# u and both gates made as Strassen column pairs behind vg, with attention outputs, normalised vg, u and gates parked in DRAM

## The chip, the cores and the metric

The kernel runs on one core of one Trainium2 chip. The metric is device time in microseconds (us) of one execution. The engines are named as in the profile: PE is the matrix engine, PEld its weight loads, DVE the vector engine, ACT the scalar engine, POOL the GpSimd engine, SP the engine that issues most DMAs; a "q" behind a name is the engine's instruction queue. POOL issues DMAs too, in its own program order.

## The reference

One transformer-like layer on x of 512 tokens by 2048 columns, in float32:

```python
h = rms_norm(x, g_mix)
q, k, v_sb, u, v_sg, gate_a, gate_b = split(h @ w_in)   # 1024,1024,1024,1024,1024,2048,2048 columns
o   = stick_breaking_attention(rms_norm(q), rms_norm(k), v_sb)     # 8 heads of 128
y_a = o @ w_oa                                                     # 1024 -> 2048
s   = gelu(u) * (W_s @ layer_norm(gelu(v_sg)) + b_s)               # mixing of 128 tokens, 8 groups
y_b = s @ w_ob                                                     # 1024 -> 2048
x   = x + (sigmoid(gate_a) * y_a + sigmoid(gate_b) * y_b) @ w_out
x   = x + square(relu(rms_norm(x) @ w_ff1)) @ w_ff2                # hidden 8192
```

## The kernel before

**Products.** Float32 operands are held as two fp32r parts, hi and lo (hi is a copy, lo the rest). A product of two such operands is three PE matmuls (`mm3`: L72 hi·hi, L73, L74), each with a moving side of up to 512 columns. Weights come by SP's queue in 512 KB pieces (`w_raw`); ACT makes `w_hi` by a copy, DVE makes `w_lo` by a subtraction (L94 and L96; L107 and L108 inside `split_to`). `w_hi` and `w_lo` share six buffers.

**Stages.** h is kept transposed (`hT`, 16 tiles of 128 rows by 512 tokens, hi and lo). In order: q, k, v for heads 0 to 3; the same for heads 4 to 7; gate a (`ga`) and y_a (`ya`) in blocks of 512 columns; `vg` (the Gelu of v_sg); u; gate b (`gb`) and y_b (`yb`); the output product `xo`; the first feed-forward product (FF1); the second. `by_token` makes a block with tokens on the partitions, `by_column` with output columns on the partitions; both take four accumulator tiles. PSUM has five such tiles for accumulators (`ps_acc`, tag "acc") and three for the rest (`ps_aux`).

**FF1** is already made in pairs of 128-column groups by a Strassen scheme over two halves of the rows, of the columns and of the tokens (`strassen_columns`). One pair of 256 columns is seven products instead of eight, on sums of weight blocks (`Sums`, made by DVE additions and by one accumulating DMA on POOL's queue, L182) and on sums of activation blocks, called factors (`y11`, `y21`, `y22`, and `m7`, `m6`, `m4`, `m5`, which `factor` makes). Six of the products use a trick of fewer matmuls: eight of 512 columns (hi and lo of the activations side by side, L214) and eight of 256 (L217). m7 has 24 of 256 columns (L72 to L74). A pair takes two accumulators (`trunk`, which carries the sum from product to product, and `side` for m7) and the three forks in `ps_aux`; ACT copies trunk into a fork (L221). The first FF1 pair is a plain one of 192 matmuls of 256 columns, since it needs no factors.

**Order.** Each engine takes its instructions in its own program order, which the tile framework's scheduler settles when the kernel is built; a waiting instruction holds everything behind it on its engine. Side work is put in a queue, `behind`: each weight piece of the main loop (`step()`) takes one entry, and `flush()` takes the rest. The attention of a half (12 entries) runs behind the next stage. `normed(tb)`, the layer norm of vg, is behind u: for each of four token blocks bn_stats (L545), r by POOL, and then for both column halves y by DVE (L554), two POOL products with the gain and bias (L556, L557), and a split into `vn`. `spatial` and `mixed` run behind gb. SBUF has 64 general slots of 128 x 512 (`slots`), 12 more until FF2 (`long`) and six weight buffers (`raws`).

## Time and profile before

| | |
|---|---|
| median of 3 runs | 2470.86 us (2469.9 to 2472.71) |
| profiled execution | 2470.69 us, its span 2469.0 us, granted clock 0.999 |
| PE busy | 2452.8 us, 99% of the span |
| DVE, ACT, POOL busy | 1625.3, 1076.4, 349.9 us |
| ga and ya | 306.8 to 588.6 us from the span's start |
| vg | 588.9 to 675.7 us |
| u | 675.9 to 762.8 us |
| gb and yb | 762.9 to 1033.0 us |
| xo | 1033.0 to 1212.8 us |
| FF1: plain pair, Strassen pairs | from 1213.0 us, from 1238.5 us to 1850.8 us |

A stage starts where the first matmul onto its tile starts. A row of a timeline gives the start in the span, the duration, the engine, the line, the operation and its tiles, and in brackets how long the engine had been idle and for whom. A matmul's row shows a longer duration than the distance to the next one, because matmuls are pipelined; the distance of starts is what one costs.

### The profile page before, as it was taken

How to read it: one execution, taken by the hardware profiler on the slowest of the kernel's cores; microseconds unless marked ns; L12 is line 12 of the kernel's file. 1: busy time of each engine (PE TensorE's matmuls, PEld its weight loads, DVE VectorE, ACT ScalarE, POOL GpSimd, SP SyncE). 2: the span in 40 equal slices, each digit the busy share in tenths (PEclk: the TensorE clock that was granted, in tenths of full speed). 3: DMA queues.
4: the chain of work that ended last, by engine and by line, in shares of the span. 5: the costliest groups of instructions: out<-in, count | busy, mean ns of one | idle time of the engine just before them, and what ended most of it. 6: DMA issues, size and time to landing. Idle time of an engine off the chain costs nothing.

```text
span 2469.0 us, 32147 instructions
## 1 busy us (share of the span) xinstructions
PE 2452.8 (99%) x12141; PEld 2078.2 (84%) x12141; DVE 1625.3 (66%) x2076; ACT 1076.4 (44%) x1521; POOL 349.9 (14%) x435
## 2 busy tenths in 40 slices
PE   9999999999999999999999999999999999999999
PEld 7888888888888888888888899888888888888887
DVE  4556463333334443334689888888888898989887
ACT  5333343122222322223377677777765443333333
POOL 0212120000030110100000000001013434312210
PEclk9999999999999999999999999999999999999999
DMA  5322322233333232434369888888895999877763
GB/s 179 94 86 70 93 77 86 94 99 97 110 101 105 93 95 94 162 128 144 97 171 235 230 232 228 225 229 229 224 290 206 309 326 295 256 227 204 248 181 95
DMA packets 349740, 416.34 MB, mean 169 GB/s; under 512 B 16992, under 2 KB 225936, under 8 KB 349584
## 3 DMA queue, kind: packets, MB, share of 16 engines
q1 hardware_dynamic: 290256, 320.41, 40.4%
q0 software_dynamic: 59040, 93.34, 16.5%
q8 instruction: 95, 1.56, 0.3%
q10 hardware_dynamic: 288, 0.52, 0.1%
q14 instruction: 61, 0.50, 0.1%
HBM read 347.10 MB, written 67.11 MB: 168 GB/s over the span
## 4 chain that ended last, share of the span: by engine, by line
PE 95%; DVE 2%; DMA 1%; issue 1%; ACT 0%; POOL 0%; DVEq 0%; SPq 0%; POOLq 0%; ACTq 0%
PE q L72 10%; PE q L73 10%; PE q L74 10%; PE q L214 7%; PE fork L214 7%; PE fork L217 4%; PE q L217 4%; PE xo L74 2%; PE xo L72 2%; PE xo L73 2%; PE gb L72 2%; PE gb L73 2%; PE gb L74 2%; PE ga L72 2%; PE ga L74 2%; PE ga L73 2%
## 5 line engine op out<-in xcount | busy, mean ns | idle before, releaser
L107 ACT CAST w_hi<-w_raw 128x1024 fp32r<-128x1024 f32 (+1 forms) x443 | 465.3, 1051 | 506.7 <-PE q L73 310.3
L108 DVE TENSOR_TENSOR w_lo<-w_raw,w_hi 128x1024 fp32r<-128x1024 f32 (+1 forms) x443 | 537.5, 1217 | 113.0 <-ACT w_hi L107 107.1
L96 DVE TENSOR_TENSOR w_lo<-w_raw,w_hi 128x1024 fp32r<-128x1024 f32 x211 | 261.7, 1240 | 523.7 <-ACT w_hi L94 519.7
L94 ACT CAST w_hi<-w_raw 128x1024 fp32r<-128x1024 f32 x211 | 221.9, 1052 | 656.7 <-PE ga L73 99.6
L73 PE MATMUL q<-w_lo,ys 128*128 128x512 f32 x896 | 349.1, 390 | 1.1 <-DVE w_lo L108 1.1
L74 PE MATMUL q<-w_hi,ys 128*128 128x512 f32 x896 | 348.6, 389 | 0.0
L72 PE MATMUL q<-w_hi,ys 128*128 128x512 f32 x896 | 312.1, 389 | 0.9 <-ACT w_hi L107 0.9
L182 POOL DMA_DIRECT2D w_raw<-in_w_ff_dram x58 | 80.9, 1396 | 905.7 <-DVE m L749 341.6
L73 PEld LDWEIGHTS q<-w_lo,ys 128*128 128x128 f32 x896 | 168.2, 188 | 37.5 <-DVE w_lo L108 2.8
L72 PEld LDWEIGHTS q<-w_hi,ys 128*128 128x128 f32 x896 | 168.1, 188 | 36.3 <-ACT w_hi L107 1.3
L74 PEld LDWEIGHTS q<-w_hi,ys 128*128 128x128 f32 x896 | 168.2, 188 | 34.8
L214 PE MATMUL q<-ys,w_hi 128*128 128x512 f32 x744 | 193.1, 395 | 2.5 <-ACT fork L221 2.5
L214 PE MATMUL fork<-ys,w_hi 128*128 128x512 f32 x744 | 186.0, 392 | 0.0
L214 PEld LDWEIGHTS fork<-ys,w_hi 128*128 128x128 f32 x744 | 136.4, 189 | 26.1
L846 POOL DMA_DIRECT2D ys<-store x224 | 127.8, 602 | 179.6 <-PE q L74 117.6
L214 PEld LDWEIGHTS q<-ys,w_hi 128*128 128x128 f32 x744 | 132.6, 190 | 24.5 <-ACT fork L221 2.7
L892 DVE SCALAR_TENSOR_TENSOR total<-q,plus,total 128x512 f32<-128x512 f32 x180 | 130.8, 743 | 0.4 <-PE q L74 0.4
L217 PEld LDWEIGHTS fork<-ys,w_lo 128*128 128x128 f32 x744 | 101.6, 190 | 7.2
L217 PEld LDWEIGHTS q<-ys,w_lo 128*128 128x128 f32 x744 | 101.1, 190 | 7.5
L217 PE MATMUL fork<-ys,w_lo 128*128 128x256 f32 x744 | 104.1, 282 | 0.0
L217 PE MATMUL q<-ys,w_lo 128*128 128x256 f32 x744 | 103.3, 281 | 0.0
L72 PE MATMUL xo<-w_hi,mT_hi 128*128 128x512 f32 x256 | 100.1, 393 | 0.0
(283 smaller groups left out, 4827.9 us busy)
## 6 DMA issues: line engine op xcount, KB each, us to landing
w_raw<-in_w_ff_dram SPq DMA_DIRECT2D x256, 512.0 KB, 5.5
w_raw<-in_w_in_dram SPq DMA_DIRECT2D x143, 512.0 KB, 3.5
ys<-store POOLq DMA_DIRECT2D x224, 256.0 KB, 6.9
w_raw<-in_w_ff_dram POOLq DMA_DIRECT2D x58, 512.0 KB, 6.9
store<-ys_hi SPq DMA_DIRECT2D x90, 256.0 KB, 4.4
store<-ys_lo SPq DMA_DIRECT2D x90, 256.0 KB, 5.4
w_raw<-in_w_out_dram SPq DMA_DIRECT2D x32, 512.0 KB, 3.7
store<-ys SPq DMA_DIRECT2D x44, 256.0 KB, 6.2
```

The costliest lines, as they stand in the source:

```text
L72: nc.tensor.matmul(o, lhsT=lh[0], rhs=rh[0], start=start, stop=False, **kw)
L73: nc.tensor.matmul(o, lhsT=lh[0], rhs=rh[1], start=False, stop=False, **kw)
L74: nc.tensor.matmul(o, lhsT=lh[1], rhs=rh[0], start=False, stop=stop, **kw)
L94: nc.scalar.copy(out=hi, in_=raw)
L96: nc.vector.tensor_tensor(out=lo, in0=raw, in1=f32(hi), op=ALU.subtract)
L107: nc.scalar.copy(out=hi, in_=src)
L108: state["lo"] = nc.vector.tensor_tensor(out=lo, in0=src, in1=f32(hi), op=ALU.subtract)
L182: nc.gpsimd.dma_start(out=self.w21, in_=self.blocks[1, 1], accum_op=ALU.add)
L214: nc.tensor.matmul(o, lhsT=hi[:, k, :], rhs=rhs[name][k], start=name == "y11" and k == 0, stop=False, skip_group_check=True)
L217: nc.tensor.matmul(o[:, :HS], lhsT=lo[:, k, :], rhs=rhs[name][k][:, :HS], start=False, stop=k == KH - 1, skip_group_check=True)
L846: nc.gpsimd.dma_start(out=f32(t), in_=store[f][HELD.index(name), p])
L892: nc.vector.scalar_tensor_tensor(out=a, in0=o, scalar=part, in1=a, op0=ALU.mult, op1=ALU.add)
```

## The change

u, gate a and gate b (5120 columns) are made in one run of 20 pairs of 256 columns that follows vg: a plain pair first, then 19 Strassen pairs, by the functions that FF1 uses (`plain_pair`, `strassen_pair`, now shared). For that `hT` is split so that the hi and lo of 256 tokens lie side by side in one tile, which makes them the factors y11 to y22 as they are. The other four factors of each of eight k come from `gate_factors`, which reads the whole h back from DRAM (`held_h`, written by `save` behind k). Their four entries follow the 12 of the second half's attention, all behind vg. The attention's outputs (`held_o`), the normalised vg (`held_v`), u and the gates (`held_g`) are written to DRAM and fetched by POOL's queue (`fetched`) when ya and yb need them. `normed` is now queued ahead of the run of pairs, `spatial` and `mixed` run behind ya.

**ACT at the end of vg.** `vg` L527 (L608 after) is the Gelu that empties a vg accumulator. Before:

```order
L94 CAST w_hi_5041<-w_raw_5039 128x1024 [waits DMAHW6_49,DVE_49,PE_49]
L527 ACTIVATE vg_4964<-vg_4720,rstd_109 128x512 [waits PE_49]
L527 ACTIVATE vg_4966<-vg_4721,rstd_109 128x512 [waits PE_49]
L527 ACTIVATE vg_4968<-vg_4722,rstd_109 128x512 [waits PE_49]
L94 CAST w_hi_5096<-w_raw_5094 128x1024 [waits DMAHW7_49,DVE_49,PE_49]
L527 ACTIVATE vg_4970<-vg_4723,rstd_109 128x512 [waits PE_49]
L94 CAST w_hi_5151<-w_raw_5149 128x1024 [waits DMAHW0_49,DVE_49,PE_49]
```

After (`ys` from `whole` are the hi parts of the factors):

```order
L94 CAST w_hi_3882<-w_raw_3880 128x1024 [waits DMAHW7_49,PE_49,Activation_49]
L110 ACTIVATE ys_3519<-whole_3516 128x256 [waits DMASW5_49,DVE_49]
L107 CAST ys_3523<-whole_3516 128x256 [waits DVE_49]
...
L107 CAST ys_3693<-whole_3676 128x256 [waits DMASW6_49,Activation_49]
L608 ACTIVATE vg_3696<-vg_3218,rstd_109 128x512 [waits Activation_49]
L608 ACTIVATE vg_3698<-vg_3219,rstd_109 128x512 [waits Activation_49]
L608 ACTIVATE vg_3700<-vg_3220,rstd_109 128x512 [waits Activation_49]
L608 ACTIVATE vg_3702<-vg_3221,rstd_109 128x512 [waits PE_49,Activation_49,Pool_49]
L94 CAST w_hi_3965<-w_raw_3963 128x1024 [waits DMAHW0_49,PE_49]
```

The Gelus of the second half stood between two weight copies; now 24 copies for the factors of six k stand between the weight copy and them.

**PE from the end of vg.** u_3712 and u_3713 are the two accumulators of the plain pair, q_4072 is the trunk of the first Strassen pair, q_4257 and q_4258 are trunk and side of the second:

```order
L74 MATMUL vg_3221<-w_hi_3628,hT_582 128x512
L72 MATMUL u_3712<-hT_149,w_hi_3716 128x256 [waits Activation_49]
...
L74 MATMUL u_3712<-hT_462,w_lo_3884 128x256
L72 MATMUL u_3713<-hT_149,w_hi_3716 128x256 [waits Activation_49]
...
L74 MATMUL u_3713<-hT_582,w_lo_3967 128x256
L214 MATMUL q_4072<-hT_149,w_hi_4074 128x512 [waits Activation_49]
...
L217 MATMUL q_4257<-hT_567,w_lo_4260 128x256
L72 MATMUL q_4258<-ys_3443,w_hi_4282 128x256 [waits DVE_49,Activation_49]
```

The second block of the plain pair waits for ACT at its first matmul, and the side tile of the second pair waits for DVE and ACT. The four vg accumulators and u_3712 are five tiles, as are u_3712, u_3713, q_4072, its side tile and q_4257.

**DVE at the emptying of u.** Before, at the end of `normed` (y is L554, u L566):

```order
L96 TENSOR_TENSOR w_lo_5374<-w_raw_5370,w_hi_5372 128x1024 [waits DMAHW2_49,PE_49,Activation_49]
L108 TENSOR_TENSOR vn_lo_5193<-y_5188,vn_hi_5192 128x512 [waits Activation_49]
L554 TENSOR_SCALAR y_5196<-vg_4970,mv_5182,r_5186 128x512
L96 TENSOR_TENSOR w_lo_5404<-w_raw_5400,w_hi_5402 128x1024 [waits DMAHW3_49,PE_49,Activation_49]
L108 TENSOR_TENSOR vn_lo_5201<-y_5196,vn_hi_5200 128x512 [waits Activation_49]
L566 TENSOR_TENSOR u_5324<-u_4980,rstd_b_110 128x512
L566 TENSOR_TENSOR u_5327<-u_4981,rstd_b_110 128x512
```

After (y is L635; L647 empties the plain pair, L275 the first Strassen pair):

```order
L108 TENSOR_TENSOR vn_lo_3875<-y_3870,vn_hi_3874 128x512 [waits Activation_49]
L635 TENSOR_SCALAR y_3943<-vg_3214,mv_3937,r_3941 128x512 [waits DMASW6_49]
...
L108 TENSOR_TENSOR vn_lo_4031<-y_4026,vn_hi_4030 128x512 [waits DMASW3_49,Activation_49]
L635 TENSOR_SCALAR y_4036<-vg_3702,mv_4020,r_4024 128x512 [waits DMASW4_49]
L108 TENSOR_TENSOR vn_lo_4041<-y_4036,vn_hi_4040 128x512 [waits Activation_49]
L647 TENSOR_TENSOR act_4046<-u_3712,rstd_b_110 128x512 [waits DMASW7_49,DMASW5_49]
L647 TENSOR_TENSOR act_4050<-u_3713,rstd_b_110 128x512 [waits DMASW6_49]
L275 TENSOR_TENSOR act_4060<-act_4060,fork_4054 128x256 [waits Activation_49]
```

The emptying of u_3712 stands behind the last `vn_lo` of `normed`, as that of u_4980 did; what is new is that PE's side tile of the second Strassen pair hangs on it, and that the weight pieces of a Strassen pair lie between the halves.

**POOL at the start of ya.** From the last accumulating weight load on; oT are the attention outputs, vn and u the inputs of `mixed`:

```order
L182 DMA w_raw_7394<-in_w_in_dram 128x8x128 [waits DMAHW0_49,DMASW0_49,DMAHW7_49,DVE_49,Activation_49]
L477 DMA oT_7581<-held_o_137 128x512 [waits PE_49]
...
L477 DMA oT_7593<-held_o_137 128x512 [waits DMASW0_49,PE_49]
L477 DMA oT_7595<-held_o_137 128x512 [waits DMASW1_49,PE_49]
L477 DMA oT_7597<-held_o_137 128x512 [waits DMASW2_49,PE_49]
L477 DMA vn_7680<-held_v_138 128x512 [waits DMASW3_49]
...
L477 DMA vn_7694<-held_v_138 128x512 [waits DMASW2_49]
L477 DMA u_7696<-held_g_139 128x512 [waits DMASW3_49]
...
L477 DMA u_7702<-held_g_139 128x512 [waits DMASW6_49]
```

Nothing of this stood on POOL's queue before; the waits on PE are for slots that the last pairs still read.

```diff
+    def plain_pair(wap, c0, ys, name):
+        o = [acc(name) for _ in range(2)]
+        for kt in range(0, KT, 4):
+            hi, lo = weight(wap, kt, c0, 2 * P)
+            for c in range(2):
+                for k in range(4):
+                    a = [part[:, k, c * P:(c + 1) * P] for part in (hi, lo)]
+                    for half in range(2):
+                        y = ys["y" + "12"[k % 2] + "12"[half], (kt + k) // 2]
+                        mm3(o[c][:, half * HS:(half + 1) * HS], a, sides(y),
+                            kt + k + half == 0, kt + k == KT - 1, skip_group_check=True)
+            step()
+        return o
...
+    def strassen_pair(wap, c0, ys, forks, loaded=True):
+        act = [slot("act"), slot("act")]
+        a11, a12, a21, a22 = (act[c][:, half * HS:(half + 1) * HS] for c in range(2) for half in range(2))
...
+    def new_forks(y):
+        forks = {}
+        for name in ("y21", "m4", "y22"):
+            forks[name] = aux("fork")
+            nc.tensor.matmul(forks[name], lhsT=y[:, :P], rhs=y, start=True, stop=True)
+        return forks
+    SIGNS = (1.0, -1.0)
...
+                parts = [both[:, 0, :], both[:, 1, :]]
             else:
-                parts = split(t, "hT", gT[:, k:k + 1], long if k < LONG // 2 else slots)
+                parts = [slot("hT", F32R, long if k < LONG // 2 else slots) for _ in range(2)]
+            for half, part in enumerate(parts):
+                split_to(part[:, :HS], part[:, HS:], t[:, half * HS:(half + 1) * HS], gT[:, k:k + 1])
             hT.append(parts)
...
+    held_h = dram.tile([KT, P, W], F32, name="held_h")
+    held_o = dram.tile([HEADS, 2, P, W], F32, name="held_o")
+    held_v = dram.tile([2, NTB, 2, P, W], F32, name="held_v")
+    held_g = dram.tile([(SGW + 2 * D) // P, P, W], F32, name="held_g")
     scale = float(P) ** -0.5
+    def fetched(src, name, dt=F32, pool=slots):
+        t = slot(name, dt, pool)
+        nc.gpsimd.dma_start(out=f32(t) if dt is F32R else t, in_=src)
+        return t
+    def save(k):
+        t = slot("whole")
+        for half, part in enumerate(hT[k]):
+            hi, lo = (f32(x) for x in sides(part))
+            nc.vector.tensor_tensor(out=t[:, half * HS:(half + 1) * HS], in0=hi, in1=lo, op=ALU.add)
+        nc.gpsimd.dma_start(out=held_h[k], in_=t)
...
-            oT[half * 4 + h] = split(o, "oT")
+            for i, part in enumerate(split(o, "oT")):
+                nc.gpsimd.dma_start(out=held_o[half * 4 + h, i], in_=f32(part))
...
+        if half == 0:
+            behind.extend([lambda k=k: [save(k + i) for i in range(4)] for k in range(0, KT, 4)])
...
-    GA = 3 * SBW + 2 * SGW
-    merged_a = []
-    ga = [gate(GA, "ga"), gate(GA + W, "ga")]
-    flush()
...
-        by_column(w_oa[0], j * W, lambda k: oT[k], SBW // P, evac_a, "ya")
...
+    hy = {}
+    def moved(k):
+        for half, part in enumerate(hT[k]):
+            name = "y" + "12"[k % 2] + "12"[half]
+            if LONG // 2 <= k < LONG // 2 + RAWH and name != "y12":
+                t = slot("hT", F32R)
+                nc.sync.dma_start(out=f32(t), in_=f32(part))
+                part = t
+            hy[name, k // 2] = part
+    def gate_factors(k):
+        whole = [fetched(held_h[2 * k + i], "whole") for i in range(2)]
+        for name in ("m7", "m6", "m4", "m5"):
+            factor(hy, whole, k, name, -1.0 if name in ("m7", "m4") else None)
+    behind.extend([lambda k=k: (moved(2 * k), moved(2 * k + 1), moved(2 * k + 2), moved(2 * k + 3),
+                                gate_factors(k), gate_factors(k + 1)) for k in range(0, KT // 2, 2)])
...
-            vn[tb, half] = split(y, "vn")
+            for i, part in enumerate(split(y, "vn")):
+                nc.gpsimd.dma_start(out=held_v[half, tb, i], in_=f32(part))
...
-    u = []
-    for half in range(2):
-        def evac_u(c, o):
-            t = slot("u")
...
-        by_column(win, 3 * SBW + half * W, hT_of, KT, evac_u, "u")
...
+    def gated(n, act, func, signs, inside):
+        for c, (t, sign) in enumerate(zip(act, signs)):
+            a = t if inside else slot("act")
+            nc.vector.tensor_tensor(out=a, in0=t, in1=rstd_b, op=ALU.mult)
+            nc.scalar.activation(out=a, in_=a, func=func, scale=sign)
+            nc.sync.dma_start(out=held_g[n + c], in_=a)
+    US, GA = 3 * SBW, 3 * SBW + 2 * SGW
+    order = [(US + n * P, n, AF.Gelu) for n in range(0, SGW // P, 2)]
+    order += [(GA + n * P, SGW // P + n, AF.Sigmoid) for n in range(0, 2 * D // P, 2)]
+    forks = None
+    for c0, n, func in order:
+        if forks is None:
+            gated(n, plain_pair(win, c0, hy, "u"), func, (1.0, 1.0), False)
+            flush()
+            forks = new_forks(hy["y11", 0])
+        else:
+            gated(n, strassen_pair(win, c0, hy, forks), func, SIGNS, True)
+    oT = [[fetched(held_o[h, i], "oT", F32R, long if h < LONG // 2 else slots) for i in range(2)]
+          for h in range(HEADS)]
...
+    def gates(which, j):
+        n = SGW // P + which * (D // P) + j * 4
+        return [fetched(held_g[n + c], "gate") for c in range(4)]
...
+    def fetch_mix(half):
+        for tb in range(NTB):
+            vn[tb, half] = [fetched(held_v[half, tb, i], "vn", F32R) for i in range(2)]
+        u.extend(fetched(held_g[half * 4 + g], "u") for g in range(4))
...
+    behind.extend([lambda: (spatial(0), fetch_mix(0)), lambda: spatial(1)])
+    behind.extend([lambda g=g: (mixed(g), fetch_mix(1) if g == 1 else None) for g in range(GROUPS)])
+    merged_a = []
+    ahead = gates(0, 0)
+    for j in range(D // W):
+        g, ahead = ahead, gates(0, j + 1) if j + 1 < D // W else gates(1, 0)
...
+        by_column(w_oa[0], j * W, lambda k: oT[k], SBW // P, evac_a, "ya")
     flush()
-    behind.extend([lambda: spatial(0), lambda: spatial(1)])
-    behind.extend([lambda g=g: mixed(g) for g in range(GROUPS)])
...
-    gb = [gate(GA + D, "gb"), gate(GA + D + W, "gb")]
...
-        g = gb.pop(0) if gb else gate(GA + D + j * W, "gb")
-        flush()
+        g, ahead = ahead, gates(1, j + 1) if j + 1 < D // W else None
```

More of the change, by code (lines that the diff above doesn't have):

```diff
@@ new lines, in tile_hybrid_layer, with __init__, __getitem__, evac @@
+    class Late:
+        def __init__(self, ys, name):
+            self.ys, self.name = ys, name
+        def __getitem__(self, k):
+            return self.ys[self.name, k]
+    def strassen_pair(wap, c0, ys, forks, loaded=True):
+        act = [slot("act"), slot("act")]
+        a11, a12, a21, a22 = (act[c][:, half * HS:(half + 1) * HS] for c in range(2) for half in range(2))
+        def evac(name, o, side):
+            a = {"y21": a11, "m4": a21, "m5": a22, "y22": a12}[name]
+            nc.scalar.copy(out=a, in_=o[:, :HS])
+            state["evac"] = nc.vector.tensor_tensor(out=a, in0=a, in1=o[:, HS:], op=ALU.add)
+            if name in ("m4", "m5"):
+                state["evac"] = nc.vector.tensor_tensor(out=a, in0=a, in1=side, op=ALU.add)
+        strassen_columns(wap, c0, {name: Late(ys, name) for name in NAMES}, forks, evac, loaded=loaded)
+        return act
@@ L419, in evac @@
             n.append(raw)
[L421 removed]
+        by_token(win, c0 + half * W, hT_at, KT, evac, name)
         def head(h):
@@ L803, in last_factors, with hidden @@
             factor(hs, x2T[2 * k:2 * k + 2], k, name, -1.0 if name == "m4" else None)
-    class Late:
-        def __init__(self, name):
-            self.name = name
-        def __getitem__(self, k):
-            return hs[self.name, k]
-    rhs = {name: Late(name) for name in NAMES}
+    def hidden(p):
+        act = strassen_pair(w_ff1[0], p * 2 * P, hs, forks, p < pairs - 1)
+        for a, sign in zip(act, SIGNS):
+            nc.scalar.activation(out=a, in_=a, func=AF.Relu, scale=sign)
+        return act
     last_factors(0)
@@ L822, in tile_hybrid_layer @@
     behind.extend([lambda k=k: two(k) for k in range(1, KT // 2, 2)])
-    def hidden(p):
-        act = [slot("relu"), slot("relu")]
-        a11, a12, a21, a22 = (act[c][:, half * HS:(half + 1) * HS] for c in range(2) for half in range(2))
-        def evac(name, o, side):
-            a = {"y21": a11, "m4": a21, "m5": a22, "y22": a12}[name]
-            nc.scalar.copy(out=a, in_=o[:, :HS])
-            state["evac"] = nc.vector.tensor_tensor(out=a, in0=a, in1=o[:, HS:], op=ALU.add)
-            if name in ("m4", "m5"):
-                state["evac"] = nc.vector.tensor_tensor(out=a, in0=a, in1=side, op=ALU.add)
-        strassen_columns(w_ff1[0], p * 2 * P, rhs, forks, evac, loaded=p < pairs - 1)
-        for a, sign in zip(act, (1.0, -1.0)):
-            nc.scalar.activation(out=a, in_=a, func=AF.Relu, scale=sign)
-        return act
     def fetch(f, name):
@@ L848, in fetch @@
         return ts
-    forks = {}
-    for name in ("y21", "m4", "y22"):
-        forks[name] = aux("fork")
-        nc.tensor.matmul(forks[name], lhsT=hs["y11", 0][:, :P], rhs=hs["y11", 0], start=True, stop=True)
+    forks = new_forks(hs["y11", 0])
     pairs = DFF // (2 * P)
```

75 lines of the change are left out of this document (26 added, 49 removed).

## The prediction

> **What bounds the kernel now.** I read the page's busy table and slices first, then the waits of PE, then the tiles of the stages that go, then single matmuls.
>
> ```profile
> PE 2452.8 (99%) x12141; PEld 2078.2 (84%) x12141; DVE 1625.3 (66%) x2076; ACT 1076.4 (44%) x1521; POOL 349.9 (14%) x435
> PE   9999999999999999999999999999999999999999
> DVE  4556463333334443334689888888888898989887
> PE 95%; DVE 2%; DMA 1%; issue 1%; ACT 0%; POOL 0%; DVEq 0%; SPq 0%; POOLq 0%; ACTq 0%
> ```
>
> PE is busy in every slice and is 95% of the chain of waits. In FF1 (slices 20 to 29) DVE is 80 to 90% busy and PE still never waits.
>
> ```profile
> PE gp L300 <- DMA gm<-in_g_mix_dram: 5.9, 1, 5.9
> PE q L214 <- ACT fork L221: 2.5, 1, 2.5
> PE q L73 <- DVE w_lo L108: 1.1, 4, 0.3
> PE q L72 <- ACT w_hi L107: 0.9, 1, 0.9
> ```
>
> These are all of PE's waits but three of 0.2 us: 5.9 us at the start, some 5 us after. So the time is PE's matmuls, and a change is worth the matmul time that it removes less every wait that it gives PE. The pitch of a matmul, from u and from an FF1 pair:
>
> ```profile
> L72 PE MATMUL u<-hT_hi,w_hi x104: 389/389/389, 675.9 to 762.3; 128*128 128x512 f32 x104
> L74 PE MATMUL u<-hT_hi,w_lo x104: 389/389/389, 676.3 to 762.7; 128*128 128x512 f32 x104
> 700.15 0.39 PE L74 MATMUL u<-hT_hi,w_lo 128*128 128x512 f32 x1
> 700.38 0.39 PE L72 MATMUL u<-hT_both,w_hi 128*128 128x512 f32 x1
> ...
> 1500.57 0.28 PE L72 MATMUL q<-ys,w_hi 128*128 128x256 f32 x1
> 1500.69 0.28 PE L73 MATMUL q<-ys,w_hi 128*128 128x256 f32 x1
> 1520.19 0.28 PE L72 MATMUL q<-ys,w_hi 128*128 128x256 f32 x1
> ```
>
> A matmul of 512 columns costs 0.226 us (u: 384 of them in 86.9 us), one of 256 costs 0.12. From m7 of one pair to m7 of the next are 19.62 us.
>
> **Matmuls removed.** u and the gates are ten blocks of 512 columns at 43.45 us, 434.5 us. In their place come a plain pair, 192 x 0.12 = 23.0, three forks, 3 x 0.226 = 0.7, and 19 pairs at 19.62 = 372.8: 396.5 us. Removed: 38.0 us. I take the FF1 pair as it is, with its waits for loads, sums and forks, because DVE has less to do here: an FF1 pair also makes and stores the factors for FF2, and a gate pair has two products with `rstd_b` of some 0.7 us instead. Attention, `mixed` and the output products keep their matmuls.
>
> **First new wait: the plain pair.** Time t runs from its first matmul. By the order, 75 matmuls of u_3712 come before u_3713, so PE is there at t = 9.0. The fifth accumulator comes free by the Gelu of vg_3218, on ACT behind 24 copies for the factors of six k; ahead of these stands `w_hi_3882`, which waits for the last vg products, so that the six k start at about t = 2 (copy 1.05, `w_lo` 1.2 after it). How DVE and ACT hand factors over is seen at FF1's start (under it the Gelu, the weight copy and rest, and a product with `rstd_b`):
>
> ```profile
> 1244.52 0.75 DVE L655 TENSOR_TENSOR x2T<-x2T 128x256 f32<-128x256 f32 x2
> 1245.30 0.41 ACT L107 CAST ys<-x2T 128x256 fp32r<-128x256 f32 x1 [2.66 <-DVE x2T L655]
> 1245.74 0.42 DVE L108 TENSOR_TENSOR ys<-x2T,ys 128x256 fp32r<-128x256 f32 x1 [0.47 <-ACT ys L107]
> 1246.08 0.42 DVE L111 SCALAR_TENSOR_TENSOR ys<-x2T,ys 128x256 fp32r<-128x256 f32 x1
> 676.82 0.68 ACT L527 ACTIVATE vg<-vg,rstd 128x512 f32<-128x512 f32 x1
> ...
> L107 ACT CAST w_hi<-w_raw 128x1024 fp32r<-128x1024 f32 (+1 forms) x443 | 465.3, 1051 | 506.7 <-PE q L73 310.3
> L108 DVE TENSOR_TENSOR w_lo<-w_raw,w_hi 128x1024 fp32r<-128x1024 f32 (+1 forms) x443 | 537.5, 1217 | 113.0 <-ACT w_hi L107 107.1
> L566 DVE TENSOR_TENSOR u<-u,rstd_b x8: 677/682/692, 722.2 to 763.1; 128x512 f32<-128x512 f32 x8
> ```
>
> Difference, copy, rest, each waiting for the one before: 0.42 + 0.41 + 0.42 and 0.03 at each hand-over, 1.3 us. m7, m6 and m4 of a k follow each other like this, since each difference overwrites the half-tile that the last one's parts are read from; m5 is independent and costs its last step: about 4.1 us a k, 24.5 for six. The Gelu ends at 2 + 24.5 + 0.68 = 27.1, and PE waits 18.1 us. From below: where nothing waits DVE starts one such instruction per 0.34 us (1245.74 to 1246.08), eight a k, 2.7 x 6 = 16.1, and the wait is 9.7. I take the long one, since the overwriting is in the code.
>
> **Second new wait: m7 of the second Strassen pair.** Its side tile needs u_3712 emptied, on DVE behind the last half of `normed`. Before, one half went like this:
>
> ```profile
> 683.54 0.68 DVE L108 TENSOR_TENSOR vn_lo<-y,vn_hi 128x512 fp32r<-128x512 f32 x1
> 684.14 0.54 DVE L554 TENSOR_SCALAR y<-vg,mv,r 128x512 f32<-128x512 f32 x1
> 684.81 1.29 POOL L556 TENSOR_TENSOR y<-y,lng 128x512 f32<-128x512 f32 x1 [2.89 <-issue]
> 686.18 1.30 POOL L557 TENSOR_TENSOR y<-y,lnb 128x512 f32<-128x512 f32 x1
> 687.70 0.62 ACT L107 CAST vn_hi<-y 128x512 fp32r<-128x512 f32 x1
> 690.26 1.29 POOL L556 TENSOR_TENSOR y<-y,lng 128x512 f32<-128x512 f32 x1 [2.79 <-DVE y L554]
> L545 DVE BATCH_NORM_STATS2 st<-vg x8: 677/694/695, 630.0 to 678.6; 128x6 f32<-128x512 f32 x8
> L182 POOL DMA_DIRECT2D w_raw<-in_w_ff_dram x58 | 80.9, 1396 | 905.7 <-DVE m L749 341.6
> L846 POOL DMA_DIRECT2D ys<-store x224 | 127.8, 602 | 179.6 <-PE q L74 117.6
> ```
>
> POOL's two L556 rows are 5.45 us apart, but that is the pace of u's weight pieces (24 x 0.226 = 5.43), whose copies stand between the halves on ACT; a half's own chain is 0.54 + 0.13 + 1.37 + 1.30 + 0.62 + 0.68 and small gaps, 4.7 us. Now POOL also issues two stores for each half, 0.6 us each; the one behind `vn_lo` comes before the next half's product: 5.3 us. Eight are 42.4; two accumulating loads of 1.4 and two fetches of oT of 0.6 stand among them: 46.4 us. It starts with the Gelus at 27.1; four bn_stats of 0.69 with their small followers, r and y take about 5: 32.4. So u_3712 is empty at about t = 78.8.
>
> Without any wait PE would be at this m7 at t = 23.0 + 0.7 + 19.6 + 2.8 (the pair's first product, eight of each kind) = 46.1. The two waits together cost 78.8 - 46.1 = 32.7 us: 18.1 in the plain pair and the rest, 14.6, here. From below, with both chains at their fast bound: 2 + 16.1 + 0.7 + 5.3 + 8 x 4.7 + 0.7 = 62.4, a cost of 16.3. From above: if each half also waits for a weight copy and its rest, 1.05 + 1.22, it takes 7.6, u_3712 is empty at t = 97.2, and the cost is 51.1. I take 32.7, since PE's long wait lets the weight pieces run ahead, and keep POOL's issues, which stand in the order.
>
> **A cold clock after the wait.** PE's first matmuls of the run, after 5.94 us without work:
>
> ```profile
> 5.94 0.25 PE L300 MATMUL gp<-ident,gm 16*128 16x16 f32 x1 [5.94 <-DMA gm<-in_g_mix_dram]
> 9.04 0.63 PE L72 MATMUL q<-w_hi,hT_hi 128*128 128x512 f32 x1
> 9.47 0.63 PE L73 MATMUL q<-w_lo,hT_hi 128*128 128x512 f32 x1
> 10.62 0.40 PE L72 MATMUL q<-w_hi,hT_hi 128*128 128x512 f32 x1
> ```
>
> They stand 0.43 us apart until 10.4 and 0.23 after: from 6.1 on some 4.3 us at about half speed, 2.1 us lost. If PE falls back so after 14 and 18 us of waiting, each wait costs 0 to 2.1 more. After the first one it hides in the second, whose end DVE and POOL set. I add 2.1 once. [...]
>
> **The start of ya.** ya used oT from SBUF; now three halves of oT, eight of vn and four of u are fetched only when the last pair lets go of the slots, and `merged_a`, which empties ya's accumulators, stands on DVE behind `sT` of `mixed`.
>
> ```profile
> ys<-store POOLq DMA_DIRECT2D x224, 256.0 KB, 6.9
> GB/s 179 94 86 70 93 77 86 94 99 97 110 101 105 93 95 94 162 128 144 97 171 235 230 232 228 225 229 229 224 290 206 309 326 295 256 227 204 248 181 95
> L621 POOL TENSOR_TENSOR smix<-smix,u x8: 1287/1293/2135, 783.7 to 830.1; 128x512 f32<-128x512 f32 x8
> ```
>
> The fetch of u is the twelfth: 12 x 0.6 + 6.9 = 14.1 us after the last pair; then POOL's product 1.29, a copy 0.62 and a rest 0.68. Two groups of `merged_a` stand behind such a step of 2.6 us: 5.2 us, my value. Below: 0, if PE has four free accumulators' work by then. Above: 3.9 MB of fetches and 4.2 MB of w_oa at the 230 GB/s of FF1 take 35 us, the last needed about 24 us after the pair: 11 us.
>
> **The rest** is hidden. `save` adds 32 DVE instructions of 0.42 us behind k and v, where DVE is 40 to 60% busy; `hT` in twice as many instructions adds 0 to 0.5 us at the very start; the stores of u and gates are two issues a pair on SP. Were SP's stores late, weight loads behind them would be late: see the rivals.
>
> **Sum**, on the profiled execution's 2470.7 (span 2469.0 and 1.7 around it; the median is 0.2 above): - 38.0 + 32.7 + 2.1 + 5.2 = + 2.0, so 2472.7; I say 2472 us.
>
> **Rivals.**
>
> *Shorter waits, faster.* Both chains run near their fast bound: 16.3 instead of 32.7, 2456 us. For it: DVE and ACT at FF1's start did run 0.34 us apart for a while, since there independent factors alternated. Against it: the overwriting, and POOL's stores.
>
> *No waits at all*, since the order is not what decides or the tile comes free otherwise: 2472.7 - 32.7 - 2.1 = 2438 us. Against it: the order names ACT and DVE at exactly these two matmuls, and there are five tiles.
>
> *DRAM decides at ya, slower.* The fetches share the DMA engines with w_oa, and the upper bound of 11 us holds: 2472.7 + 5.8 = 2478.5. It decides once the last oT or vn lands more than 24 us after the last pair. For it: 6.9 us of landing was measured at 230 GB/s. Against it: the slices of FF2 reach 326 GB/s.
>
> **Numbers.** A measurement of this kernel tells 0.2%, 4.9 us, from no change: 2465.9 to 2475.8. The forecast, no change, 0.38; shorter waits 0.28; no waits 0.04; DRAM at ya 0.22; 0.08 for a wait I have not seen (a late store on SP's queue among them), slower. Faster 0.32, same 0.38, slower 0.30. Likeliest alone: 2464 to 2478. The range, which reaches into both neighbours: 2454 to 2486.
>
> **What would show it.** In the changed profile: PE's waits with one of about 18 us at the first u_3713 matmul behind ACT's Gelu, and one of about 15 at an m7, behind DVE's L647; matmuls 0.24 us apart instead of 0.12 for some 4 us after them; 19.6 us from m7 to m7 from the third pair on; POOL's products of `normed` 5 to 7 us apart; a few us of waiting for `merged_a` at ya. I am wrong if the first wait is under 12 us (then the factors don't chain), if pairs are longer than 20 us, or if ya loses more than 11.

## The result, and the profile after

The changed kernel takes 2494.17 us (median of 5 runs, 2492.42 to 2495.54) against 2469.9 us of the kernel before (5 runs, 2467.83 to 2472.71): a ratio of 1.0097, 95% interval 1.0082 to 1.0112. It is slower by 24 us; the forecast was 2472 us and its range ended at 2486. The profiled execution has a span of 2492.4 us and a granted clock of 0.987 (before: 2469.0 and 0.999).

The busy table of the changed kernel, and its slices of PE and of the granted clock:

```profile
PE 2428.3 (97%) x12696; PEld 2087.2 (84%) x12696; DVE 1848.0 (74%) x2416; ACT 1196.2 (48%) x1759; POOL 467.9 (19%) x590
PE   9999998699999989999999999999999999999999
PEclk9999999899999989999999999999999999999999
```

PE now has three slices that are not full: 7 and 8 (374 to 498 us), where the run of pairs starts, and 15 (872 to 935 us), where ya does. The clock dips in two of the three. The largest waits of PE (who waited for whom; us in total, times, the longest):

```profile
PE q L72 <- DVE act L647: 18.6, 1, 18.6
PE u L72 <- ACT vg L608: 15.6, 1, 15.6
PE gp L366 <- DMA gm<-in_g_mix_dram: 5.9, 1, 5.9
PE ya L72 <- DVE merged_a L737: 5.0, 2, 2.5
PE mix L717 <- DVE smix L723: 3.9, 2, 2.2
PE wsT L685 <- DMA ws<-in_w_spatial_dram: 2.6, 1, 2.6
PE q L214 <- ACT fork L221: 2.5, 1, 2.5
PE u L72 <- DMA hT<-hT_both: 2.1, 1, 2.1
PE ya L74 <- DVE w_lo L96: 1.1, 1, 1.1
```

All waits together are 58.9 us, before 11.0: 47.9 more. PE's busy time fell by 24.5 us and not by the 38.0 of the removed matmuls, which leaves 13.5 us. -38.0 + 47.9 + 13.5 = +23.4, as the span grew; this is only busy and idle time added up again, so it has to close. That the 13.5 us are matmuls at a lower clock is seen in their starts: the slow stretches named below make up some 12 of it. So two things have to be explained, the waits and the slow matmuls.

Where they lie follows from a few starts on PE. The first matmul of the plain pair is at 415.07 us. The two large waits, in PE's timeline (start, duration; in brackets the idle time before and for whom):

```profile
423.77 0.35 PE L72 MATMUL u<-hT,w_hi 128*128 128x256 f32 x1 [2.10 <-DMA hT<-hT_both]
...
443.73 0.58 PE L72 MATMUL u<-hT,w_hi 128*128 128x256 f32 x1 [15.60 <-ACT vg L608]
444.11 0.42 PE L73 MATMUL u<-hT,w_hi 128*128 128x256 f32 x1
...
449.27 0.28 PE L74 MATMUL u<-hT,w_lo 128*128 128x256 f32 x1
449.39 0.28 PE L72 MATMUL u<-hT,w_hi 128*128 128x256 f32 x1
...
501.76 0.55 PE L72 MATMUL q<-ys,w_hi 128*128 128x256 f32 x1 [18.64 <-DVE act L647]
```

The plain pair ends its first wait at t = 28.7 and m7 of the second Strassen pair starts at t = 86.7, where 46.1 was the figure without any wait: 40.6 us lost up to there. From then on the pairs run as in FF1: m7 starts again at 523.8 us and its 24 L72 matmuls of three pairs reach to 565.5, two pitches of 19.6 us. ya starts at 851.7 and xo at 1057.7 us, a stretch of 206.0 us; less its waits and slow matmuls it is 187 (below). xo came at 1033.0 us before, so all of the difference lies ahead of it.

### The profile page after: what moved, and what is told of

Same layout as the page of the kernel before. It is cut to its first block, busy times and chain, and to the rows that moved or that the text cites. A ratio compares the mean times of both kernels' runs of the same rounds, so it can differ in the third digit from the quotient of the medians.

```text
span 2492.4 us, 34437 instructions
## 1 busy us (share of the span) xinstructions
PE 2428.3 (97%) x12696; PEld 2087.2 (84%) x12696; DVE 1848.0 (74%) x2416; ACT 1196.2 (48%) x1759; POOL 467.9 (19%) x590
## 4 chain that ended last, share of the span: by engine, by line
PE 61%; DVE 1%; DMA 0%; issue 0%; ACT 0%; POOL 0%; DVEq 0%
PE q L72 9%; PE q L73 9%; PE q L74 9%; PE q L214 7%; PE fork L214 7%; PE fork L217 4%; PE q L217 4%; PE xo L72 2%; PE xo L74 2%; PE xo L73 2%; PE yb L74 1%; PE yb L73 1%; PE yb L72 1%; PE ya L72 1%; PE ya L73 1%; PE ya L74 1%
## 5 line engine op out<-in xcount | busy, mean ns | idle before, releaser
L107 ACT CAST w_hi<-w_raw 128x1024 fp32r<-128x1024 f32 (+1 forms) x576 | 604.8, 1050 | 661.1 <-PE q L73 339.7
L108 DVE TENSOR_TENSOR w_lo<-w_raw,w_hi 128x1024 fp32r<-128x1024 f32 (+1 forms) x576 | 704.9, 1227 | 169.9 <-ACT w_hi L107 160.2
L96 DVE TENSOR_TENSOR w_lo<-w_raw,w_hi 128x1024 fp32r<-128x1024 f32 x135 | 168.9, 1251 | 243.1 <-ACT w_hi L94 239.1
L94 ACT CAST w_hi<-w_raw 128x1024 fp32r<-128x1024 f32 x135 | 141.8, 1050 | 373.0 <-issue 78.3
L72 PE MATMUL q<-w_hi,ys 128*128 128x512 f32 x896 | 312.0, 389 | 0.9 <-ACT w_hi L107 0.9
L214 PE MATMUL q<-ys,w_hi 128*128 128x512 f32 x1048 | 268.4, 393 | 2.5 <-ACT fork L221 2.5
L214 PE MATMUL fork<-ys,w_hi 128*128 128x512 f32 x896 | 224.9, 393 | 0.0
L214 PEld LDWEIGHTS q<-ys,w_hi 128*128 128x128 f32 x1048 | 186.9, 189 | 34.1 <-ACT fork L221 2.7
L72 PEld LDWEIGHTS q<-w_hi,ys 128*128 128x128 f32 x896 | 168.1, 188 | 36.2 <-ACT w_hi L107 1.3
L217 PEld LDWEIGHTS q<-ys,w_lo 128*128 128x128 f32 x1048 | 142.5, 190 | 10.4
L217 PE MATMUL q<-ys,w_lo 128*128 128x256 f32 x1048 | 145.7, 282 | 0.0
L72 PE MATMUL q<-ys,w_hi 128*128 128x256 f32 x400 | 114.4, 286 | 18.6 <-DVE act L647 18.6
```

Of the source, the lines that this page charges most:

```text
L72: nc.tensor.matmul(o, lhsT=lh[0], rhs=rh[0], start=start, stop=False, **kw)
L94: nc.scalar.copy(out=hi, in_=raw)
L96: nc.vector.tensor_tensor(out=lo, in0=raw, in1=f32(hi), op=ALU.subtract)
L107: nc.scalar.copy(out=hi, in_=src)
L108: state["lo"] = nc.vector.tensor_tensor(out=lo, in0=src, in1=f32(hi), op=ALU.subtract)
L214: nc.tensor.matmul(o, lhsT=hi[:, k, :], rhs=rhs[name][k], start=name == "y11" and k == 0, stop=False, skip_group_check=True)
```

## The experiments

The reasons to test were these. The order theory (A): the two large waits are only a matter of where the factors and `normed` are queued, and go when these are queued later. Its rival (B): DVE, ACT and POOL have to get through this work before the pairs can run on, so the wait moves to the next one in need of it. After the first four runs a third was formed (C): the 64 general slots are full, and what empties an accumulator waits for slots that `normed` holds until its halves are stored. Beside them: what the DVE and POOL do to each other, what the clock costs, and what holds ya. Runs without an interval are single executions; the kernel before measured 2468.55 to 2469.48 on the same chips, and the changed kernel scatters by up to 1.8 us around its median.

**Late factors (1).** Only the factors of k = 0 and 1 stay behind vg, the other six are queued behind the plain pair, ahead of `normed`:

```diff
-                                gate_factors(k), gate_factors(k + 1)) for k in ...
+                                gate_factors(k) if k == 0 else None, ...
+    behind.extend([lambda k=k: (gate_factors(k), gate_factors(k + 1)) for k in range(2, KT // 2, 2)])
     behind.extend([lambda tb=tb: normed(tb) for tb in range(NTB)])
```

> Edit: only the factors of the first two k are made behind vg; those of the other six are queued behind the plain pair, so that the Gelus which empty vg come ahead of them. Theory A (each wait is a matter of what stands ahead of an emptied tile, and each costs its own length and some 2.5 us of half clock after it): the 15.6 us wait in the plain pair and its slow matmuls go; the emptying of u now stands behind two halves of the layer norm and not eight, so that the 18.6 us wait goes too; the first m7 waits about 5 us for its last factor: 2452 to 2462 us. Theory B (the 24 us of factors and 50 us of layer norm have to pass DVE, ACT and POOL ahead of the pairs in any case, the waits only move): 2480 to 2494 us, with a long wait at the first or second m7.

2501.44 us, above both forecasts. The plain pair has no wait left, and PE waits later and longer. The largest of these waits:

```profile
PE q L214 <- ACT fork L221: 35.8, 4, 29.2
PE q L72 <- ACT ys L110: 5.4, 3, 2.0
```

and ACT's timeline there, the last copy of `normed` and then the emptying of the first Strassen pair (L274), behind which PE's next fork (L221) stands:

```profile
514.36 0.62 ACT L107 CAST vn_hi<-y 128x512 fp32r<-128x512 f32 x1 [4.23 <-POOL y L639]
514.88 0.36 ACT L274 COPY act<-fork 128x256 f32<-128x256 f32 x1
515.14 0.38 ACT L274 COPY act<-q 128x256 f32<-128x256 f32 x1
515.41 0.66 ACT L274 COPY act<-fork 128x256 f32<-128x256 f32 x2
516.06 0.57 ACT L221 COPY fork<-q 128x512 f32<-128x512 f32 x1
```

The emptying stands behind all eight halves; that its tiles (`act`) come from slots which are free only when halves of vn are in DRAM is argued here, and tried in the run with the norm in place. Theory A falls: moved work takes its wait along.

**Late norm (2), and both late (3).** `normed` behind the emptying of the plain pair; then also the late factors:

```diff
-    behind.extend([lambda tb=tb: normed(tb) for tb in range(NTB)])
...
             forks = new_forks(hy["y11", 0])
+            behind.extend([lambda tb=tb: normed(tb) for tb in range(NTB)])
```

> Edit: the layer norm of vg is queued behind the emptying of the plain pair, not ahead of it. Theory A: the wait of 18.6 us at the second m7 goes with its 2.5 us of half clock, the wait in the plain pair stays: 2470 to 2476 us. Theory B: the layer norm's instructions stand in the second and third pair's way and PE waits for weight rests instead, in sum as long: 2485 to 2494 us.

> Edit: both of the above. Theory A: both waits gone but for about 5 us at the first m7: 2450 to 2460 us, no more than 5 us below the first edit alone. Theory B: 2475 to 2494 us.

2494.2 and 2496.86 us, both just above what B allowed. In the first of them u is emptied at once and the wait for L647 is gone, but PE waits 22.3 us for forks (longest 14.9) where it had waited 2.5; in the other 31.7 us. No place in the order removes the wait.

**Norm in place.** The y of `normed` overwrites vg, which nothing else reads: eight slots fewer.

```diff
-            y = slot("y")
+            y = t
```

> Edit: on the changed kernel, the layer norm writes y over its vg tile and takes no slot of its own; all instructions stay. The first four runs let the wait of PE move and not vanish, so two theories stand. Theory B (throughput: DVE, ACT and POOL must pass factors and layer norm first): no gain, 2491 to 2496 us. Theory C (the 64 slots of SBUF are full of hT, 32 factors and vg, so that the tiles into which u and the first pair are emptied come free only when halves of the layer norm have been stored): with one slot less per half the emptying stands behind six halves, not eight, and the second wait of 18.6 us loses some 8 to 10: 2482 to 2488 us.

2480.29 us, 14 less, of which 7.6 lie in the run of pairs (from the first matmul of u to that of ya 429.0 us instead of 436.6) and 3.7 at ya. No PE wait for L647 is left; two of PE's waits, and DVE's row of the eight y:

```profile
PE u L72 <- ACT vg L608: 16.4, 1, 16.4
PE u L74 <- DVE w_lo L96: 7.7, 1, 7.7
```

```profile
445.48 13.12 DVE L635 TENSOR_SCALAR vg<-vg,mv,r 128x512 f32<-128x512 f32 x8
```

This is what theory C says of the second wait. The change takes no operation away; with slots at hand DVE makes all eight y in a row, where in the changed kernel each y stands behind the `vn_lo` of the half ahead of it (the orders shown under "The change" have it: y and the emptying of u wait for DMAs of POOL's queue there, DMASW, and for none in the kernel before). 7.7 us come back as a new wait: `w_lo` of the plain pair now stands on DVE behind those y, which take 13.1 us beside POOL's products where eight at their usual 0.54 would take 4.3.

**Norm on DVE.** The two products with gain and bias go from POOL to DVE:

```diff
-            nc.gpsimd.tensor_tensor(out=y, in0=y, in1=lng[half], op=ALU.mult)
-            nc.gpsimd.tensor_tensor(out=y, in0=y, in1=lnb[half], op=ALU.add)
+            nc.vector.tensor_tensor(out=y, in0=y, in1=lng[half], op=ALU.mult)
+            nc.vector.tensor_tensor(out=y, in0=y, in1=lnb[half], op=ALU.add)
```

> Edit: on the changed kernel, the layer norm's two products (gain, bias) are made by DVE instead of POOL. In the changed kernel's trace DVE's 128x1024 subtractions take 2.2 to 2.3 us where they lie beside a POOL product, 1.2 elsewhere, and POOL's products 1.9 to 2.15 beside them, 1.29 alone. If the two engines slow each other there, the 2.2 us rows vanish and the second wait shrinks by 6 to 10 us, also since a half needs no hand-over to POOL: 2482 to 2488 us. If the stores' slots alone decide, 2490 to 2495 us.

2484.68 us, 9.5 less; the second wait is 10.0 us instead of 18.6. DVE makes such a product in 0.69 us, so the run alone does not tell a faster engine from an undisturbed one; but its subtractions of 128x1024 are back at 1.22 us. Why POOL's products are slow is seen in the changed kernel, DVE's timeline and then POOL's over the same 6 us:

```profile
464.17 1.21 DVE L108 TENSOR_TENSOR w_lo<-w_raw,w_hi 128x1024 fp32r<-128x1024 f32 x1
465.41 2.20 DVE L186 TENSOR_TENSOR w_raw<-w_raw 128x1024 f32<-128x1024 f32 x1
467.53 2.31 DVE L108 TENSOR_TENSOR w_lo<-w_raw,w_hi 128x1024 fp32r<-128x1024 f32 x1
```

```profile
464.65 1.88 POOL L637 TENSOR_TENSOR y<-y,lng 128x512 f32<-128x512 f32 x1
466.61 2.15 POOL L638 TENSOR_TENSOR y<-y,lnb 128x512 f32<-128x512 f32 x1
```

By these rows they take turns here. POOL's first product begins at 464.65 and ends at 466.53, 1.15 us after DVE's subtraction (465.38); DVE's next one, from 465.41, ends 1.08 us after that product (467.61 after 466.53); POOL's second ends 1.15 us after it (468.76), and DVE's last 1.08 us after that. In the kernel before such a subtraction takes 1.22 (DVE) and such a product 1.29 us (POOL), 0.14 us more than these distances. In the best version below there are no such turns.

**Warm clock.** 70 matmuls whose result nothing reads stand behind the first matmuls of the plain pair, so that PE is idle for less of its first wait:

> Edit: on the changed kernel, 70 matmuls of 512 columns without a use (15.8 us) stand in PE's order behind the first 24 of the plain pair, so that PE works through most of what was its first wait. Nothing else is changed; the tile that they write is read by nobody. If the half clock comes from PE's idling, the granted clock stays at 1.00 through the plain pair, its matmuls behind the wait stand 0.12 us apart and not 0.21, and only the second wait is followed by slow ones; the time stays within 2 us of the changed kernel (2492 to 2496), since the end of the second wait is set by the layer norm and its stores, not by PE. If the slow clock has another cause, the matmuls stay 0.21 apart.

2491.64 us, 2.5 less. The first wait is 3.3 us. Up to it and for 1 us behind it the clock stays up (matmuls 0.12 us apart), then it falls all the same (0.21 us apart), from 444.1 to 447.5 us:

```profile
443.09 0.39 PE L72 MATMUL u<-hT,w_hi 128*128 128x256 f32 x1 [3.32 <-ACT vg L612]
443.31 0.28 PE L73 MATMUL u<-hT,w_hi 128*128 128x256 f32 x1
...
444.51 0.41 PE L73 MATMUL u<-hT,w_hi 128*128 128x256 f32 x1
444.73 0.41 PE L74 MATMUL u<-hT,w_lo 128*128 128x256 f32 x1
```

So the expectation that no slow matmul follows the first wait was missed: after 3.3 us of waiting they stand 0.21 us apart here too. The second wait is 18.8 us and ends at t = 86.6 (86.7 in the changed kernel), when DVE has emptied the tile; slow matmuls ahead of it cost nothing, as the prediction had it. The 2.5 us lie elsewhere, 2.2 of them between ya and xo.

**The start of ya: mixing later, weights earlier.** In one run `spatial` and `mixed` stand three steps further behind ya's fetches; in the other the spatial weights `ws` and `bs` are asked for at the ninth of the 20 pairs, not behind the last one (n counts groups of 128 columns, two a pair, so n = 16 is not the seventeenth pair, as the expectation has it; `ws` is issued at 607.9 us instead of 848.2):

```diff
-    behind.extend([lambda: (spatial(0), fetch_mix(0)), lambda: spatial(1)])
+    behind.extend([lambda: fetch_mix(0), lambda: None, lambda: None, lambda: spatial(0), lambda: spatial(1)])
```

```diff
+        if n == 16:
+            load_ws()
```

> Edit: on the changed kernel as it is, the fetches for the spatial mixing are queued as before, but the spatial weights and the mixing follow three steps of ya later. If ya loses its 20 us by the order in which the mixing's short chain (PE, DVE, POOL, ACT, DVE) stands ahead of the emptying of ya, and by the late spatial weights, half of it goes: 2480 to 2486 us. If the DMA engines set the pace there (they move 370 to 400 GB/s for 35 us), nothing changes: 2491 to 2496 us.

> The changed kernel with one edit: the spatial weights and biases (ws, bs) are asked for at the seventeenth Strassen pair and no longer behind the last one's ref. The wait wsT <- DMA ws of 2.6 us must go. If the late weights are what costs the start of ya its 20 us (everything of the mixing stands behind them in TensorE's order), the time is 2483 to 2489. If it is the order of the mixing's own steps (sT, mix, merged_a, each released by VectorE a step late), only the wait itself goes, and the time is 2490 to 2494.

Later mixing: 2484.79 us, 9.4 less; ya to xo 196.0 instead of 206.0 us; the wait for `smix` is gone, that for `merged_a` is 3.7, that for `ws` 3.4. Early weights, in 4 runs: 2489.05 us (2487.73 to 2490.42; to before 1.0081, 1.0065 to 1.0096), 5.1 less; ya to xo 202.0; the wait for `ws` is gone, those for `merged_a` (5.0) and `smix` (4.3) are as they were. Half of the 5.1 is the wait itself, and the time falls between the two forecasts. So the larger part is the order of the mixing's own steps, each of which PE asks for before DVE has it, and late weights the smaller.

The clock has its part in it. The windows of PE in the changed kernel (stretch, its length, busy us and matmuls, granted clock, DMA share, GB/s):

```profile
850.00:860.00 10.00, 10.00 (x52) 1.00 1.03 378
860.00:870.00 10.00, 7.40 (x29) 0.83 1.04 376
870.00:880.00 10.00, 8.92 (x42) 1.00 1.04 396
...
890.00:900.00 10.00, 6.46 (x21) 0.66 0.61 203
...
920.00:930.00 10.00, 5.25 (x26) 0.85 0.37 115
930.00:940.00 10.00, 10.00 (x38) 0.81 0.06 24
```

Busy time by the missing clock, 7.40 x 0.17 + 6.46 x 0.34 + 5.25 x 0.15 + 10.00 x 0.19, is 6.1 us; with 12.6 of waits 18.7 are lost, and 187.3 remain. In the last version below the same sum gives 196.5 - 7.4 - 2.2 = 186.9: the same is left of both, so waits and clock explain the difference.

**More plain pairs.** Three plain pairs, `normed` behind the first, the factors one k a step behind the second and third; then the same with the mixing later:

```diff
-    forks = None
+    forks, done_plain, PLAINS = None, 0, 3
...
-            flush()
-            forks = new_forks(hy["y11", 0])
+            done_plain += 1
+            if done_plain == 1:
+                flush()
+                behind.extend([lambda k=k: gate_factors(k) for k in range(KT // 2)])
```

> Edit: three plain pairs instead of one; the layer norm runs behind the first, while the factors do not yet hold 32 slots, and the factors behind the second and third. Each plain pair costs 23.0 instead of 19.6 us, 6.8 for two more. Theory C: the emptyings find free slots, no long wait is left in the run; the 36.3 us of waits there and some 8 us of half clock go: 2454 to 2462 us. Theory B: 69 us of plain pairs do not cover 24 and 50 us of side work and the weight pieces: a wait of 10 to 20 us is left at the first m7, 2468 to 2480 us.

> Edit: the three plain pairs, and at ya the spatial weights and the mixing five steps later than in the change. By the run with the mixing three steps later (9.4 us gained) ya loses another 9 to 14 us of its 20: 2442 to 2452 us, if the order at ya and the run of pairs are independent; if the gain at ya only came from what the waits ahead had left prefetched, as the run above.

2487.76 and 2481.93 us, both above their forecasts. A plain pair costs 3.4 us more than a Strassen pair, so three give up 6.8 of the 38.0. The plain pairs run without a wait, but 19 us of waits stand in the first Strassen pairs, for the factors (8.8 for `ys` from DVE, 5.2 from ACT, 4.9 for forks): the fetches of h stand on POOL's queue behind the stores of `normed` and behind fetches of oT, which wait for slots that PE still reads.

**Fewer slots, and factors in turn.** First y in place and the norm stored whole, split only after it is fetched (no slot for the two parts, eight stores instead of 16), with the mixing six steps late. Then, on top of it, the factors of two k in turn, six of the eight k behind the plain pair; then the same with two plain pairs:

```diff
-            for i, part in enumerate(split(y, "vn")):
-                nc.gpsimd.dma_start(out=held_v[half, tb, i], in_=f32(part))
+            nc.gpsimd.dma_start(out=held_v[half, tb], in_=y)
```

```diff
-    def gate_factors(k):
+    def gate_factors(*ks):
...
         for name in ("m7", "m6", "m4", "m5"):
-            factor(hy, whole, k, name, -1.0 if name in ("m7", "m4") else None)
+            for k in ks:
+                factor(hy, whole[k], k, name, -1.0 if name in ("m7", "m4") else None)
```

> Edit: on the changed kernel with its one plain pair, y is written over its vg tile and stored as it is, one store per half and no split (the split is made behind the fetch at ya), and the mixing comes six steps later. The layer norm then takes no slot at all. Theory C (slots): the emptying of u and of the first pair never waits for a store; the second wait shrinks from 18.6 us to under 6, and with some 10 us from ya: 2464 to 2472 us. Theory B (the chain's throughput): POOL's products alone take 8 x 2.6 = 21 us behind the Gelus at t = 28, so that a second wait of 10 us or more stays: 2474 to 2482 us.

> Edit: as the run before it, and the factors of two k are made in turn, m7 of the one, m7 of the other, and so on, so that no instruction waits for its own predecessor; those of k 2 to 7 are queued behind the plain pair, behind the Gelus. Theory C: the factors take about 17 us instead of 24.5 and are there when the first m7 comes at t = 26.5; neither long wait is left: 2440 to 2452 us. If factors, layer norm and weight pieces are too much for DVE and ACT in 50 us whatever their slots (theory B): 2460 to 2475 us.

> Edit: as the run before it, with two plain pairs (3.4 us more of matmuls, 23 us more of cover). Theory C: 2442 to 2454 us, about 3 us above the run with one plain pair if that had no wait, below it if it had. Theory B: the cover is what counts, 10 us or more below the run with one plain pair.

2481.12, 2473.82 and 2459.51 us. The second wait is gone in the first, and 14.9 us for vg's Gelus and 7.4 for a `w_lo` remain; the second takes these away and has waits of 5.2 us for a weight copy, 4.6 for a factor and several shorter ones in their place; the second plain pair gives DVE and ACT 23 us more, and the time falls by 14.3 us although the pair costs 3.4. All three came out as theory B has it and not as C does. PE's waits between the first matmul of u and that of ya tell how far each goes: 36.3 us in the changed kernel, 29.6 with the norm in place, 28.8 with it stored whole, 17.8 with the factors in turn, 6.7 with the second plain pair. So slots explain the second wait, and the greater part is work that needs time on DVE, ACT and POOL. Only with slots free, factors in turn and time for them is the gain of the matmuls left over.

**The best version in five runs**, with early `ws` added; and the same with the mixing three steps late instead of six:

> The kernel of the two plain pairs with the factors of two k made in turn, normed stored whole and the mixing six steps late (2459.5 in one look), with the same edit as the run beside it. If the ws wait of 3.0 us there is only itself, 2456 to 2458; if it also holds up the mixing behind it, 2445 to 2454. Against the kernel before, by the theory that slots and not arithmetic cost the change its gain: faster by 0.4 to 1%; by the rival, that the run of Strassen pairs itself costs what it saves: within 0.2%.

> As the run ahead of it, with the mixing three steps late instead of six. If merged_a is what the start of ya waits for, this is 2 to 8 us slower than the run ahead of it; if the fetches of the halves (oT, vn, gates, u) are late because of their sheer bytes, both are within 2 us of each other.

2457.48 us (2455.72 to 2458.36) against 2468.86 us: ratio 0.9953, 95% interval 0.994 to 0.9965. It is faster than both kernels. The other is at 2456.13 us in one run, no different. By its expectation that speaks for late fetches, but in neither run does PE wait for a fetch behind the start of ya; the waits there are 7.4 and 8.2 us, most of them for `smix` and `merged_a`. Busy time and all waits above 1 us of the first:

```profile
PE 2424.7 (99%) x12768; PEld 2087.1 (85%) x12768; DVE 1848.4 (75%) x2404; ACT 1191.2 (49%) x1749; POOL 446.6 (18%) x573
```

```profile
PE gp L366 <- DMA gm<-in_g_mix_dram: 5.8, 1, 5.8
PE u L74 <- DVE w_lo L96: 4.1, 1, 4.1
PE q L214 <- ACT fork L221: 3.2, 2, 2.5
PE mix L723 <- DVE smix L729: 3.0, 1, 3.0
PE ya L72 <- DVE merged_a L743: 1.9, 1, 1.9
PE q L214 <- DVE ys L108: 1.8, 1, 1.8
PE yb L72 <- DVE merged_a L743: 1.7, 1, 1.7
```

All its waits are 23.8 us, 12.8 more than before, where the changed kernel had 47.9 more. The wait for `w_lo` is a matter of DVE and POOL again. POOL has six independent products in a row there, and the subtraction beside them gets no turn: it takes 11.17 us instead of 1.22 and ends 1.09 us after the last of them (DVE's row, then POOL's):

```profile
425.02 11.17 DVE L96 TENSOR_TENSOR w_lo<-w_raw,w_hi 128x1024 fp32r<-128x1024 f32 x1
```

```profile
419.42 7.73 POOL L638 TENSOR_TENSOR vg<-vg,lng 128x512 f32<-128x512 f32 x6
427.65 7.45 POOL L639 TENSOR_TENSOR vg<-vg,lnb 128x512 f32<-128x512 f32 x6
```

Its matmuls save 38.0 - 3.4 = 34.6 us, and its span is 15.2 us shorter than that of the kernel before: the rest is waits and clock. So the run of Strassen pairs does save what its matmuls say, and in the changed kernel waits and clock took it.

## Why the prediction was wrong, step by step

*Matmuls removed, -38.0:* right. Pairs from the third on stand 19.6 us apart as FF1's.

*First wait, end at t = 27.1:* right by its end, 28.7, and by who is waited for: the Gelu of vg behind ACT's 24 copies, which are 417.76 to 442.70 us. The wait that it names is 15.6 instead of 18.1, because PE reached it later than t = 9.0: it had waited 2.1 us for a DMA that copies parts of `hT` into place, which the prediction left out, and ran at half clock after it (granted clock 0.53 from 425.0 to 428.2 us). The same end is reached, so that this cost nothing.

*Second wait, u_3712 empty at t = 78.8:* the chain that it names is the one that PE waits for, and its size was too small. PE went on at t = 86.7; the two waits cost 40.6 us instead of 32.7, inside the bounds of 16.3 and 51.1. The term that was too small is the 46.4 us of the eight halves. Their first product began at t = 33.3 (32.4 predicted), but they followed each other every 6.96 us, POOL's other issues included, and DVE began to empty u 52.6 us later:

```profile
L637 POOL TENSOR_TENSOR y<-y,lng x8: 1269/1863/1891, 448.3 to 497.0; 128x512 f32<-128x512 f32 x8
L638 POOL TENSOR_TENSOR y<-y,lnb x8: 1261/1918/2163, 450.8 to 498.4; 128x512 f32<-128x512 f32 x8
```

(least, median and largest duration in ns.) The prediction took 1.29 and 1.30 us for these products from the kernel before, where DVE was busy for 30 to 40% of the time; beside the weight differences of the run of pairs they take 1.86 and 1.92 us in the median, and DVE's differences beside them 2.20 and 2.31 us (464 to 470 us) instead of 1.22. All sixteen took 27.3 us instead of 20.7, and these 6.6 us more than cover the 6.2 that the halves took longer; the rest of the 7.9 is the later start (0.9) and the emptying itself, which the sum left out (0.8). Moving the products to DVE gave 8.6 us of the wait back. What the prediction did not see at all is why the eight halves stand in a row: for slots. The step treated the emptying of u as late only through DVE's order; with eight slots more the wait for it goes, though not all of the time.

*A cold clock, 2.1 once:* too small. It is right that the slow matmuls after the first wait hide in the second; after the second 24 matmuls stand 0.21 us apart instead of 0.12, which loses 2.4. But the term knew of two waits only, and PE also falls to half clock at ya (granted clock 0.66 from 890 to 900 us, products of 512 columns 0.43 us apart instead of 0.23): 6.1 us more. So of the slow matmuls some 3.6 us ahead of the second wait are hidden, and some 8.5 are paid.

*The start of ya, 5.2, at most 11:* this is the step that failed most. The stretch lost 18.7 us, 12.6 of waits and 6.1 of clock. `merged_a` behind `sT` was expected and costs 5.0. The other waits were not: the mixing's matmuls for `smix` (3.9), for late spatial weights (2.6) and `w_lo` (1.1). The step priced one chain, fetch to `merged_a`, and left out that PE's own order now has `spatial` and `mixed` between ya's matmuls, where every missing input stops everything behind it. The prediction's own test ("if ya loses more than 11") says wrong here. DRAM, the rival for this place, did run at 376 to 396 GB/s in the first 30 us, but the later mixing takes 10 us off the stretch with the same fetches, and the best version moves up to 397 GB/s there without a wait of PE for a fetch, so it is not what decides.

*The sum:* -38.0 + 40.6 + 2.4 + 18.7 = 23.7 against 23.4 measured in the span. Of the 21.7 us that the forecast of +2.0 lacked, 13.5 are ya, 7.9 the two waits and 0.3 the clock after them. The rivals that made it faster were not met; the reason that was held against them, the waits, was too weak by these terms. The chance of 0.30 for slower rested mostly (0.22) on DRAM at ya, the wrong mechanism for the right place, and reached 2478.5 us only.

What stays open: no run frees the slots and takes the products off POOL at once, so it is not shown whether the 7.7 us that came back with the norm in place would go then.

## What to carry to other kernels

When a stage is replaced by one with fewer matmuls, list what it must hold at the same time, against the buffers that there are: here full slots put eight halves in a row that PE waited for, and moving the work in the order only moved the wait. Then ask whether the other engines have the time for it: freeing the slots alone gave back 7.6 us in the run of pairs, factors in turn and a second plain pair some 20 more. Price an instruction from a row in which its neighbours on the other engines are what they will be, not from one in which they had less to do (POOL's product with the gain took 1.29 us in the kernel before, 1.86 in the changed one); and price the start of each following stage by PE's own order, one missing input at a time. A long wait of PE can cost more than its length: behind the one of 18.6 us the matmuls stood 0.21 us apart instead of 0.12 for 5.3 us, which cost 2.4; what followed the one of 15.6 us was hidden by the next wait.
